# Weight-stream matmuls in groups of eight blocks instead of pairs

## The chip, the cores and the metric

The kernel runs on one core of one Trainium2 chip. The metric is the device time of one launch in microseconds, from three runs of the kernel before: median 2434.75 us (2434.34 to 2435.21).

## The reference, cut to what matters

Two layers of a decoder run over 256 tokens of width 2048, in float32. Each layer computes `h = rmsnorm(x)`, one input projection, four token mixers (softmax attention, gated short convolution, Conformer convolution, retention), an output projection, a gated MLP of width 5632 with a causal convolution of three taps, and a gated input:

```
z = h @ w_in                        # 2048 x 4928, split among the four mixers
y = concat(y_a, y_b, y_c, y_d);  x = x + y @ w_o             # 2048 x 2048
uf = dwconv(rmsnorm(x) @ w_up, w_ffn_conv)                   # 2048 x 11264
gate, up = split(uf);  x = x + (silu(gate) * up) @ w_down    # 5632 x 2048
x = x + (p @ w_pe) * sigmoid(rmsnorm(x) @ w_pg)              # 2048 x 2048
```

Every one of these products reads its weights once, since all 256 tokens fit into one pass.

## The kernel before, in words

Features lie on the partitions, tokens in the free dimension. All weights come as one stream of 128x128 blocks in the order in which TensorE takes them (`layer_plan`, line 38). The stream arrives in raw tiles of 16 blocks (queue SP, line 267, three buffers). Halves of eight blocks are converted in `conv_to` (line 260): ScalarE copies the raw float32 half to a rounded tile `hi` (line 272), VectorE subtracts to get the rest, `lo` (line 273). There are four buffers of each, and a half is converted two halves ahead of its use (`PF`, line 217).

Activations are held the same way: a tile `xs[k]` of 512 columns holds the rounded values of the 256 tokens in its first half and the rest in its second half. A product of float32 exactness is then `hi*x_hi + hi*x_lo + lo*x_hi`. With `ab` true, `linear` (line 292) does it with two matmuls for each block: `hi` against all 512 columns (a wide one) and `lo` against the first 256 columns (a narrow one), which adds into the second half of the same PSUM bank. Each of the two loads its own 128x128 block into the array first. The two halves of the bank are added when the result is evacuated (`evac`, line 339, and `x_add`, line 874).

`linear` runs over K input tiles and `nmt` output tiles (two, as a rule); the two output tiles lie in two banks of the accumulator `acc`, of which there are two. In the order before, wide and narrow alternate block by block; in the last k of a product the narrow one comes first. With `ab` false (the products of `do_up` and `w_pe`, and the last two of `w_pg`) a block takes three narrow matmuls. `linear_nat` (line 321) is another form: tokens are stationary and 512 columns of weights move, so all its matmuls are wide.

In each layer the products with `ab` true are: 17 of `w_in` (K = 16; one of them, `zkr`, has one output tile), 16 of `w_o` (K = 8, first over eight y tiles, then over the other eight), 44 of `w_up` (K = 16), 16 of `w_down` (K = 22), and seven of `w_pg` (K = 16). That makes 3152 blocks a layer.

The work of the mixers and norms is put between the matmuls of the stream as background (`Bg`, line 144): after each k `linear` calls `bg.tick()`, which advances each chain by its rate. A chain's TensorE and VectorE instructions are kept behind the stream's last instruction (`Paced`, line 122). Engines take their instructions in program order, so a background matmul that waits holds up the stream.

Of the kernel before, what the change touches and what calls it, by code (L numbers as in the profile page):

```python
# [17 lines left out]
P = 128  # L18
D = 2048
S = 256  # L20
# [13 lines left out]
CF_RATE = 0.4  # L34
HB = 8


def layer_plan():
    """Blocks of the weight stream of one layer, in the order the tensor engine takes them:
    (matrix, first row, columns)."""  # L40
    blocks = []

    def group(mat, ks, cols):
        for k in ks:
            for c in cols:
                blocks.append((mat, k * P, c))

    r = lambda a: np.arange(a, a + P)
    ks = range(KD)
    for kind, cols in in_groups():  # L50
        if kind == "up":
            up_cols = lambda h: r(h * 192)
            rope = lambda j: np.concatenate(
                [np.arange((2 * j + s) * 192 + 128, (2 * j + s) * 192 + 192) for s in (0, 1)])
            for a in (0, 2):
                group("w_kv_up", range(2), [r(h * 256) for h in (a, a + 1)])
            group("w_kv_up", range(2), [r(h * 256 + 128) for h in range(4)])
            for a in (0, 2):
                group("w_q_up", range(4), [up_cols(a), up_cols(a + 1)])
            group("w_q_up", range(4), [rope(0), rope(1)])  # L60
        else:
            group("w_in", ks, cols)
    for ys in (YORD, YLAST):
        for m in range(0, KD, 2):
            group("w_o", ys, [r(m * P), r((m + 1) * P)])
    for half in range(2):
        h0 = half * (NFF // 2)
        for j in range(h0, h0 + NFF // 2):
            group("w_up", ks, [r(j * P), r(DFF + j * P)])
        for m in range(0, KD, 2):  # L70
            group("w_down", range(h0, h0 + NFF // 2), [r(m * P), r((m + 1) * P)])
    for m in range(0, KD, 2):
        group("w_pe", range(2), [r(m * P), r((m + 1) * P)])
        if m + 2 < KD:
            group("w_pg", ks, [r(m * P), r((m + 1) * P)])
        else:
            group("w_pg", ks, [r(m * P)])
            group("w_pg", ks, [r((m + 1) * P)])
    return blocks
# [26 lines left out]

# columns of the array of per-channel vectors
def vec_plan():
# [13 lines left out]
class Paced:  # L122
    """An engine whose instructions, while the background runs, keep their place behind the
    main stream's last instruction on it."""

# [18 lines left out]
class Bg:  # L144
    """Work that is put between the groups of the main matmul stream."""

# [4 lines left out]
    def add(self, chain, rate, gen):  # L151
        """Queue gen on a chain that advances rate steps for every step of the main stream."""
        c = self.chains.setdefault(chain, [rate, deque(), 0.0])
        c[0] = rate
        c[1].append(gen)
# [30 lines left out]
def trunk(ctx: ExitStack, tc: tile.TileContext, ws, xT, pT, pos, vec, dec, ident_d, rope_c, out):  # L186
# [3 lines left out]
    V, T = Paced(tc, nc.vector, state), Paced(tc, nc.tensor, state)  # L190
# [3 lines left out]
    one = ctx.enter_context(tc.tile_pool(name="one", bufs=1))  # L194
# [16 lines left out]

# [1 line left out]
    vt = one.tile([P, L * NV], F32, tag="vt", name="vt")  # L213
# [44 lines left out]

# [1 line left out]
    def conv_to(h):  # L260
# [28 lines left out]
    bg = Bg(state)  # L289

# [1 line left out]
    def linear(xs, nmt, ab, ps=None, pre=None):  # L292
# [4 lines left out]
        else:  # L297
            t = None
        for k in range(K):
            if pre is not None:  # L300
                pre(k)
            for m in range(nmt):
                hi, lo = blk()
                f, l = k == 0, k == K - 1
                xk = xs[k]
                if ab:
                    if not l:
                        T.matmul(ps[m], hi, xk, start=f, stop=False)
                        T.anchor = T.matmul(ps[m][:, S:2 * S], lo, xk[:, 0:S], start=False, stop=False).ins
                    else:  # L310
                        T.matmul(ps[m][:, S:2 * S], lo, xk[:, 0:S], start=False, stop=False)
                        T.anchor = T.matmul(ps[m], hi, xk, start=False, stop=True).ins
                else:
                    T.matmul(ps[m][:, 0:S], hi, xk[:, 0:S], start=f, stop=False)
                    T.matmul(ps[m][:, 0:S], hi, xk[:, S:2 * S], start=False, stop=False)
                    T.anchor = T.matmul(ps[m][:, 0:S], lo, xk[:, 0:S], start=False, stop=l).ins
            bg.tick()
        return t

# [1 line left out]
    def linear_nat(xs):  # L321
# [38 lines left out]

# [1 line left out]
    def sm(n):  # L362
        return tl("s8", [P, n], F32, 24)

    def col_sums(ps, c0, srcs):
        """Sums over partitions of every [rows, S] in srcs (with the column that weighs its rows)."""
        for tt in range(2):
# [26 lines left out]
    def row_gen(hl, c0=0):  # L394
        """The values of a column pair [P, 2] (tokens on the partitions) as a row on every partition."""
        dg = tl("dg", [P, 2, 2, P], F32R, 2)
# [12 lines left out]

# [1 line left out]
    def rope_tables():  # L411
# [33 lines left out]
    def rope(dst, src, n, ct, sn, tag):  # L445
        """dst, src [P, n, S]: two heads of 64 rows on the partitions, halves of 32 rows."""
        sw = tl(tag, [P, n, S], F32, 3)
# [5 lines left out]

# [1 line left out]
    class Norm:  # L455
# [36 lines left out]
    def tiles(which, n):  # L492
        """which: 0, 1 the two sets of 16 split tiles, 2 the six spare ones."""
        return [tl("S%d_%d" % (which, i), [P, 512], F32R) for i in range(n)]
# [3 lines left out]

    # ================= one layer =================
    def layer_fwd(li, nrm, a, nxt):  # L500
        """nrm: the norm before the mixers, its split tiles in set a; nxt: set of the next layer."""
        b = 1 - a
# [7 lines left out]

# [1 line left out]
        def t_zkv(z):  # L512
# [175 lines left out]

# [1 line left out]
        cfu = [None, None]  # L690
# [49 lines left out]

# [1 line left out]
        def t_rot(z, key, sl):  # L742
# [43 lines left out]

# [1 line left out]
        scv = {}  # L788
# [81 lines left out]

# [1 line left out]
        AB = True  # L872
# [28 lines left out]

# [1 line left out]
        n3 = None  # L903
# [27 lines left out]

# [1 line left out]
        nn = norm_begin(li + 1, "g_mix", tiles(b, 16)) if li + 1 < L else None  # L933
# [31 lines left out]
def _host(inputs):  # L965
# [36 lines left out]
    vec = vec.reshape(P, L * NV)  # L1002
    # constants of the shapes
    k = np.arange(P)[:, None, None].astype(np.float64)
# [29 lines left out]
```

## Time and profile before

| what | value |
|---|---|
| median of three runs | 2434.75 us |
| span of the profiled execution | 2433.3 us |
| outside the span, against the median | about 1.45 us |
| PE busy | 2413.8 us (99%), 13808 matmuls |
| PEld busy | 2095.6 us (86%) |
| VectorE busy | 1765.3 us (73%) |
| ScalarE busy | 1321.7 us (54%) |
| HBM over the span | 181 GB/s, DMA engines 50.6% on the weight queue |

PE is TensorE's matmul row and PEld its weight loads, which overlap. The end of a matmul is modelled, and matmuls are pipelined, so the busy time of PE counts overlaps and its mean duration (394 ns for a wide one on the page) isn't what one costs. What one costs is read from the start of one to the start of the next. In a timeline row, "x2" means that two alike were merged, and the row gives the start of the first.

### The profile page before, as it was taken

What the parts mean: (1) busy time and instruction counts of PE and PEld (TensorE: products, weight loads), DVE (VectorE), ACT (ScalarE), POOL (GpSimd) and SP (SyncE); (2) the same over time, 40 slices, a digit from 0 to 9 for tenths busy, and PEclk for the clock granted to TensorE, in tenths of its full rate; (3) what the DMA queues carried; (4) which work ended last, traced back from release to release, by engine and by line L of the source; (5) the groups of instructions that cost most, each with busy time, mean ns of one, the idle gap of its engine ahead of it and who ended that gap; (6) DMA issues with size and microseconds to landing.
All of it is one profiled execution on the core that took longest, in us unless ns stands there. A gap on an engine that the chain in (4) does not pass through costs nothing.

```text
span 2433.3 us, 34793 instructions
## 1 busy us (share of the span) xinstructions
PE 2413.8 (99%) x13808; PEld 2095.6 (86%) x13808; DVE 1765.3 (73%) x2722; ACT 1321.7 (54%) x1896; POOL 11.5 (0%) x35
## 2 busy tenths in 40 slices
PE   8999999999999999999999999999999999999999
PEld 6888888888888888888888888888888888888888
DVE  7977978777556777666788788877775567776565
ACT  6665566555434555545556655655554355555453
POOL 0000000000000000000000000000000000000000
PEclk9999999999999999999999999999999999999999
DMA  6544555555555555555554445555555555555553
GB/s 245 183 147 143 190 180 184 191 191 178 188 189 190 187 179 189 191 183 182 189 185 170 149 144 189 191 186 188 181 191 190 184 184 187 190 188 181 186 200 129
DMA packets 63331, 443.33 MB, mean 182 GB/s; under 512 B 7248, under 2 KB 7504, under 8 KB 10304
## 3 DMA queue, kind: packets, MB, share of 16 engines
q1 hardware_dynamic: 62640, 439.39, 50.6%
q8 instruction: 108, 1.77, 0.3%
q0 software_dynamic: 528, 1.73, 0.2%
q14 instruction: 55, 0.45, 0.1%
HBM read 438.99 MB, written 2.10 MB: 181 GB/s over the span
## 4 chain that ended last, share of the span: by engine, by line
PE 95%; DVE 3%; ACT 1%; DMA 0%; issue 0%; SPq 0%; DVEq 0%; ACTq 0%
PE acc L133 92%; PE ps L133 3%; DVE lo L133 1%; DVE cfu L133 1%; DMA x<-xT 0%; DVE e L133 0%; ACT hi L272 0%; DVE s L133 0%; DVE m L133 0%; DVE S L133 0%; ACT dg L399 0%; DVE tabsm L133 0%; DVE tabsr L133 0%; DVE nacc L133 0%; ACT m L667 0%
## 5 line engine op out<-in xcount | busy, mean ns | idle before, releaser
L133 PE MATMUL acc<-S,hi 128*128 128x512 f32 x6560 | 2268.1, 394 | 11.5 <-DVE S L133 11.2
L133 PE MATMUL acc<-S,lo 128*128 128x256 f32 x6432 | 1777.4, 281 | 0.8 <-DVE lo L133 0.8
L133 PEld LDWEIGHTS acc<-S,hi 128*128 128x128 f32 x6560 | 1213.5, 188 | 283.3 <-DVE S L133 12.5
L133 DVE TENSOR_TENSOR lo<-raw,hi 128x1024 fp32r<-128x1024 f32 x830 | 1014.5, 1222 | 451.2 <-ACT hi L272 449.5
L133 PEld LDWEIGHTS acc<-S,lo 128*128 128x128 f32 x6432 | 1216.7, 189 | 19.7 <-DVE lo L133 1.9
L272 ACT CAST hi<-raw 128x1024 fp32r<-128x1024 f32 x830 | 869.8, 1048 | 625.4 <-PE acc L133 572.0
L342 ACT COPY e<-acc 128x512 f32<-128x512 f32 x138 | 80.5, 583 | 231.0 <-PE acc L133 231.0
L133 DVE TENSOR_TENSOR e<-acc,e 128x512 f32<-128x512 f32 x138 | 94.7, 686 | 127.7 <-ACT e L342 127.7
L133 DVE SCALAR_TENSOR_TENSOR m<-e,vt,m 128x255 f32<-128x255 f32 (+1 forms) x352 | 146.1, 477 | 0.0
L133 DVE SCALAR_TENSOR_TENSOR cfu<-cfpad,vt,cfu 128x256 f32<-128x256 f32 x240 | 115.4, 481 | 1.5
L915 ACT ACTIVATE m<-e,vt 128x256 f32<-128x256 f32 x176 | 80.1, 502 | 47.3 <-DVE e L133 47.3
L133 DVE TENSOR_TENSOR e<-e,rrow 128x512 f32<-128x512 f32 x138 | 94.7, 687 | 4.0
L877 ACT COPY e<-acc 128x512 f32<-128x512 f32 x64 | 37.5, 586 | 79.5 <-PE acc L133 79.3
L133 DVE TENSOR_TENSOR x<-x,acc 128x512 f32<-128x512 f32 x64 | 43.9, 686 | 40.3 <-ACT e L877 40.3
L920 ACT ACTIVATE m<-m 128x256 f32<-128x256 f32 x88 | 36.8, 418 | 46.7 <-DVE m L133 46.7
L133 DVE TENSOR_TENSOR x<-x,e 128x512 f32<-128x512 f32 (+1 forms) x82 | 55.6, 678 | 2.3
L133 PE MATMUL acc<-hi,S 128*128 128x512 f32 x144 | 47.1, 397 | 0.0
L357 ACT ACTIVATE S<-x,vt 128x256 fp32r<-128x256 f32 x96 | 42.9, 495 | 1.8 <-DMA x<-xT 1.8
L133 DVE SCALAR_TENSOR_TENSOR S<-x,vt,S 128x256 fp32r<-128x256 f32 x96 | 42.0, 479 | 0.9 <-ACT S L357 0.9
L133 DVE TENSOR_TENSOR S<-m,S 128x256 fp32r<-128x256 f32 x92 | 38.3, 418 | 0.0
L133 DVE TENSOR_TENSOR m<-m 128x256 f32<-128x256 f32 x90 | 37.8, 420 | 0.0
L353 ACT CAST S<-m 128x256 fp32r<-128x256 f32 x92 | 36.3, 397 | 0.0
(161 smaller groups left out, 686.9 us busy)
## 6 DMA issues: line engine op xcount, KB each, us to landing
raw<-ws SPq DMA_DIRECT2D x413, 1024.0 KB, 4.8
raw<-ws SPq DMA_DIRECT2D x4, 512.0 KB, 9.9
x<-xT SPq DMA_DIRECT2D x8, 256.0 KB, 10.5
out<-x SPq DMA_DIRECT2D x7, 256.0 KB, 2.3
dect<-dec POOLq DMA_DIRECT2D x1, 512.0 KB, 10.1
m<-pT POOLq DMA_DIRECT2D x4, 128.0 KB, 3.0
vt<-vec POOLq DMA_DIRECT2D x1, 466.0 KB, 8.6
out<-x SPq DMA_DIRECT2D x2, 128.0 KB, 1.7
```

What stands on the lines that cost most here:

```text
L133: r = fn(*a, **k)
L272: A.copy(his[i], src)
L342: A.copy(out_, t[:, 0:nmt, S:2 * S])
L353: A.copy(dst[:, 0:S], src)
L357: A.activation(dst[:, 0:S], src, AF.Identity, scale=g)
L877: A.copy(e, t[:, :, S:2 * S])
L915: A.activation(y[:, m], u[:, m], AF.Identity, scale=w(2))
L920: A.activation(y[:, 0], y[:, 0], AF.Silu)
```

## The change: groups of up to eight blocks

With `ab` true and no `pre` callback, `linear` now takes the blocks in groups of `GRP` = 8 (four k for two output tiles): first the wide matmuls of all blocks of the group, then their narrow ones. In the last group of a product the narrow ones come first. The first product of the first layer (which has a `pre`) and all products with `ab` false keep their order. The background is ticked after every `2 * nmt` matmuls, so as many times in a product as before. The number of matmuls, weight loads, conversions and DMAs stays the same.

```
+GRP = 8
...
-        for k in range(K):
+        step = GRP // nmt if ab and pre is None else 1
+        for k0 in range(0, K, step):
+            ks = range(k0, min(k0 + step, K))
             if pre is not None:
-                pre(k)
-            for m in range(nmt):
-                hi, lo = blk()
-                f, l = k == 0, k == K - 1
-                xk = xs[k]
-                if ab:
-                    if not l:
-                        T.matmul(ps[m], hi, xk, start=f, stop=False)
-                        T.anchor = T.matmul(ps[m][:, S:2 * S], lo, xk[:, 0:S], start=False, stop=False).ins
-                    else:
-                        T.matmul(ps[m][:, S:2 * S], lo, xk[:, 0:S], start=False, stop=False)
-                        T.anchor = T.matmul(ps[m], hi, xk, start=False, stop=True).ins
-                else:
+                pre(k0)
+            w = [(k, m, blk()) for k in ks for m in range(nmt)]
+            if not ab:
+                for k, m, (hi, lo) in w:
+                    f, l, xk = k == 0, k == K - 1, xs[k]
...
-            bg.tick()
+                bg.tick()
+                continue
+            last = ks[-1] == K - 1
+
+            def wide():
+                for k, m, (hi, lo) in w:
+                    yield ps[m], hi, xs[k], k == 0, k == K - 1
+
+            def narrow():
+                for k, m, (hi, lo) in w:
+                    yield ps[m][:, S:2 * S], lo, xs[k][:, 0:S], False, False
+
+            n = 0
+            for part in ((narrow, wide) if last else (wide, narrow)):
+                for o, wt, xk, f, l in part():
+                    T.anchor = T.matmul(o, wt, xk, start=f, stop=l).ins
+                    n += 1
+                    if n % (2 * nmt) == 0:
+                        bg.tick()
```

On TensorE, before, the end of a product of `w_down` (K = 22, accumulator `acc_9563`) and the start of the next read as follows. `hi` and `lo` are the halves of the weight stream, `S` the activation tiles; 128x512 is a wide matmul and 128x256 a narrow one.

```order
L133 MATMUL acc_9563<-S_4_1082_6962,hi_9616 128x512
L133 MATMUL acc_9563<-S_4_1082_6962,lo_9617 128x256
L133 MATMUL acc_9563<-S_4_1082_6962,hi_9616 128x512
L133 MATMUL acc_9563<-S_4_1082_6962,lo_9617 128x256
L133 MATMUL acc_9563<-S_5_1083_6963,lo_9617 128x256
L133 MATMUL acc_9563<-S_5_1083_6963,hi_9616 128x512
L133 MATMUL acc_9563<-S_5_1083_6963,lo_9617 128x256
L133 MATMUL acc_9563<-S_5_1083_6963,hi_9616 128x512
L133 MATMUL acc_9689<-S_0_1062_6942,hi_9636 128x512
L133 MATMUL acc_9689<-S_0_1062_6942,lo_9637 128x256
```

The same place after the change, where "x2" stands for the two output tiles:

```order
L134 MATMUL acc_9563<-S_2_1080_6960,lo_9609 128x256 x2
L134 MATMUL acc_9563<-S_3_1081_6961,lo_9609 128x256 x2
L134 MATMUL acc_9563<-S_4_1082_6962,lo_9609 128x256 x2
L134 MATMUL acc_9563<-S_5_1083_6963,lo_9609 128x256 x2
L134 MATMUL acc_9563<-S_4_1082_6962,hi_9608 128x512 x2
L134 MATMUL acc_9563<-S_5_1083_6963,hi_9608 128x512 x2
L134 MATMUL acc_9689<-S_0_1062_6942,hi_9628 128x512 x2
L134 MATMUL acc_9689<-S_1_1063_6943,hi_9628 128x512 x2
L134 MATMUL acc_9689<-S_2_1064_6944,hi_9628 128x512 x2
L134 MATMUL acc_9689<-S_3_1065_6945,hi_9628 128x512 x2
L134 MATMUL acc_9689<-S_0_1062_6942,lo_9629 128x256 x2
L134 MATMUL acc_9689<-S_1_1063_6943,lo_9629 128x256 x2
```

Wide and narrow matmuls now stand in runs, and since the last group of a product begins with the narrow ones and the next product with the wide ones, runs also meet at both ends of the last group.

On TensorE, before, where the first norm's row (`ps_315<-dg_310`, a background product of two matmuls) stands at the end of the second product of `w_in` and the start of the third:

```order
L133 MATMUL acc_327<-S_14_18_137,hi_353 128x512
L133 MATMUL acc_327<-S_14_18_137,lo_354 128x256
L133 MATMUL ps_315<-dg_310,ones_r 128x256
L133 MATMUL acc_327<-S_14_18_137,hi_353 128x512
L133 MATMUL acc_327<-S_14_18_137,lo_354 128x256
L133 MATMUL acc_327<-S_15_19_138,lo_354 128x256
L133 MATMUL acc_327<-S_15_19_138,hi_353 128x512
L133 MATMUL acc_327<-S_15_19_138,lo_354 128x256
L133 MATMUL acc_327<-S_15_19_138,hi_353 128x512
L133 MATMUL acc_427<-S_0_4_123,hi_377 128x512
L133 MATMUL ps_315<-dg_310,ones_r 128x256
L133 MATMUL acc_427<-S_0_4_123,lo_378 128x256
```

And after:

```order
L134 MATMUL acc_327<-S_14_18_137,hi_353 128x512 x2
L134 MATMUL acc_327<-S_15_19_138,hi_353 128x512 x2
L134 MATMUL acc_427<-S_0_4_123,hi_377 128x512 x2
L134 MATMUL ps_315<-dg_310,ones_r 128x256
L134 MATMUL acc_427<-S_1_5_124,hi_377 128x512 x2
L134 MATMUL ps_315<-dg_310,ones_r 128x256
L134 MATMUL acc_427<-S_2_6_125,hi_377 128x512 x2
L134 MATMUL acc_427<-S_3_7_126,hi_377 128x512 x2
L134 MATMUL acc_427<-S_0_4_123,lo_378 128x256 x2
L134 MATMUL acc_427<-S_1_5_124,lo_378 128x256 x2
```

The two background matmuls now fall into a run of wide ones, about three blocks later in the stream than before.

On ScalarE, before, around the evacuation of one product of `w_up` (`e<-acc`); `hi<-raw` is the conversion of a half, the `m` rows are the convolution and the gate, `S_10` is the rounded half of an activation tile:

```order
L272 CAST hi_8065<-raw_7985 128x1024
L342 COPY e_8049<-acc_7964 128x512
L272 CAST hi_8087<-raw_8027 128x1024
L915 ACTIVATE m_8053<-e_8049,vt 128x256 x2
L272 CAST hi_8107<-raw_8027 128x1024
L920 ACTIVATE m_8053<-m_8053 128x256
L272 CAST hi_8129<-raw_8085 128x1024
L353 CAST S_10_1072_6952<-m_8053 128x256
L272 CAST hi_8165<-raw_8085 128x1024
```

And after:

```order
L273 CAST hi_8065<-raw_7985 128x1024
L355 COPY e_8049<-acc_7964 128x512
L273 CAST hi_8087<-raw_8027 128x1024
L273 CAST hi_8107<-raw_8027 128x1024
L928 ACTIVATE m_8053<-e_8049,vt 128x256 x2
L273 CAST hi_8129<-raw_8085 128x1024
L933 ACTIVATE m_8053<-m_8053 128x256
L366 CAST S_10_1072_6952<-m_8053 128x256
L273 CAST hi_8165<-raw_8085 128x1024
```

One conversion has moved ahead of the convolution; the number of conversions that stand ahead of the evacuation is the same.

## Rows read from the trace of the kernel before

**Rows 1.** The page: span, busy times, and granted TensorE clock in 40 slices.
```profile
span 2433.3 us, 34793 instructions
...
PE 2413.8 (99%) x13808; PEld 2095.6 (86%) x13808; DVE 1765.3 (73%) x2722; ACT 1321.7 (54%) x1896; POOL 11.5 (0%) x35
...
PEclk9999999999999999999999999999999999999999
```

**Rows 2.** The page: the chain that ended last, shares by engine.
```profile
PE 95%; DVE 3%; ACT 1%; DMA 0%; issue 0%; SPq 0%; DVEq 0%; ACTq 0%
```

**Rows 3.** Waits of PE: for whom, us in total, times, longest.
```profile
PE acc L133 <- DVE S L133: 11.2, 3, 8.4
PE ps L133 <- DVE m L133: 1.0, 3, 0.6
PE ps L133 <- ACT dg L399: 0.9, 3, 0.3
PE acc L133 <- DVE lo L133: 0.8, 2, 0.6
```

**Rows 4.** Groups of instructions by shape: count, busy us, mean ns, idle before.
```profile
L133 PE MATMUL acc<-S,hi 128*128 128x512 f32 x6304 | 2221.9, 399 | 11.3 <-DVE S L133 11.2
L133 PE MATMUL acc<-S,lo 128*128 128x256 f32 x6432 | 1777.4, 281 | 0.8 <-DVE lo L133 0.8
```

**Rows 5.** The chain in order of time: start us, us, what, merged count.
```profile
254.66 27.45 PE acc L133 x156
...
385.00 734.93 PE acc L133 x4163
...
1147.65 11.31 PE acc L133 x64
...
1590.27 734.93 PE acc L133 x4163
```

**Rows 6.** Timeline of PE in a `w_up` product: start us, us, instruction.
```profile
1000.04 0.40 PE L133 MATMUL acc<-S,hi 128*128 128x512 f32 x1
1000.27 0.28 PE L133 MATMUL acc<-S,lo 128*128 128x256 f32 x1
1000.39 0.40 PE L133 MATMUL acc<-S,hi 128*128 128x512 f32 x1
...
1009.93 0.40 PE L133 MATMUL acc<-S,hi 128*128 128x512 f32 x1
```

**Rows 7.** Timeline of PE in `linear_nat` of layer one (wide matmuls alone).
```profile
172.11 0.61 PE L133 MATMUL acc<-hi,S 128*128 128x512 f32 x2
172.56 0.39 PE L133 MATMUL acc<-lo,S 128*128 128x512 f32 x1
...
175.51 0.39 PE L133 MATMUL acc<-hi,S 128*128 128x512 f32 x1
```

**Rows 8.** Timeline of PE in the last `w_pg` product (narrow matmuls alone).
```profile
2416.49 0.40 PE L133 MATMUL acc<-S,hi 128*128 128x256 f32 x2
...
2424.77 0.40 PE L133 MATMUL acc<-S,hi 128*128 128x256 f32 x2
```

**Rows 9.** Timeline of PE: wide matmuls that follow a run of narrow ones.
```profile
1312.43 0.40 PE L133 MATMUL acc<-hi,S 128*128 128x512 f32 x1
...
1312.90 0.62 PE L133 MATMUL acc<-hi,S 128*128 128x512 f32 x2
...
1314.27 0.62 PE L133 MATMUL acc<-hi,S 128*128 128x512 f32 x2
```

**Rows 10.** Timeline of PE: narrow matmuls (`w_pe`) that follow a wide one.
```profile
1119.77 0.39 PE L133 MATMUL ps<-p,hi 128*128 128x256 f32 x2
...
1120.71 0.28 PE L133 MATMUL ps<-p,lo 128*128 128x256 f32 x1
```

**Rows 11.** Timeline of PE in a `w_in` product: alternating pairs, first and last.
```profile
182.25 0.39 PE L133 MATMUL acc<-S,hi 128*128 128x512 f32 x1
...
184.68 0.39 PE L133 MATMUL acc<-S,hi 128*128 128x512 f32 x1
```

## The prediction

> **What bounds the kernel now.** I read the page first: PE is busy for 99% of the span and no other engine over 73%, and every slice of the granted clock shows 9, the top digit: the level of 2.4 GHz throughout [rows 1]. The chain that ended last lies on PE for 95% of the span [rows 2]. So I asked next what PE waits for: 11.2 us for activation tiles, with one wait of 8.4 us, which is the load of x at the start, and under 3 us for everything else, the converted weights among it [rows 3]. In the MLP the chain is PE without a break for 734.93 us in each layer [rows 5]. Weights, DMA and evacuation are hidden there; the time is the number of matmuls times the distance from one start to the next, and the change can act only through that distance or through new waits.
>
> The shapes give the number: 6304 wide matmuls with `hi`, as many as the code has blocks with `ab` true (2 x 3152), and one narrow one for each [rows 4]. Their mean times (399 and 281 ns) are modelled and overlap, so I leave them and take starts. Alternating, 28 pairs take 1009.93 - 1000.04 = 9.89 us, 353.2 ns a pair [rows 6]; over the whole MLP stage it is 734.93 / 4163 x 2 = 353.1 ns [rows 5].
>
> Then I looked for places where the kernel already does what the change will do. `linear_nat` issues wide matmuls alone, each with its own weight load: 15 of them take 175.51 - 172.11 = 3.40 us, 226.7 ns each [rows 7]. The last product of `w_pg` issues narrow ones alone: 69 take 2424.77 - 2416.49 = 8.28 us, 120.0 ns each [rows 8]. The sum is 346.7 ns, 6.4 ns less than an alternating pair costs in the MLP. Alternation isn't slow everywhere: in one product of the mixers seven pairs take 184.68 - 182.25 = 2.43 us, 347.1 ns [rows 11]. I read this as two rhythms into which an alternating stream can fall, a quick one that costs as much as the pure runs and a slow one, and nearly all of the MLP stands in the slow one. A pure run shows one steady distance alone.
>
> **What a group costs.** A run doesn't settle at once. Eight wide ones that follow narrow ones take 1314.27 - 1312.43 = 1.84 us, 0.026 more than eight settled ones (the row at 1314.27 is the ninth start) [rows 9]. Eight narrow ones right behind a wide one take 1120.71 - 1119.77 = 0.94 us, 0.02 less than eight settled ones [rows 10]. A turn from narrow to wide and back so costs 0.006 to 0.01 us net; I take 0.007. Eight blocks then cost 1.84 + 0.94 = 2.78 us against 8 x 0.3531 = 2.825. The wide runs of rows 9 are those of `linear_nat`, with tokens stationary; I assume that which operand is weights makes no difference. The bounds: without any cost of the turn 2.773; with the late start of the wide ones but no relief for the narrow ones 1.84 + 0.96 = 2.80.
>
> **The sum.** A product with K = 16 has four groups; since its last group is narrow first, it has three turns; with K = 22 (five groups and a half one) five, with K = 8 one.
>
> - `w_up`, 88 products: 32 x 0.3467 + 3 x 0.007 = 11.115 us against 32 x 0.3531 = 11.299: -0.184 each, -16.2.
> - `w_down`, 32 products of 44 pairs: 15.290 against 15.536: -0.246 each, -7.9.
> - `w_pg`, 14 products: 11.115 against 11.31 [rows 5]: -2.7.
> - `w_o`, 32 products of 16 pairs at 27.45 / 156 x 2 = 0.3519 [rows 5]: 5.554 against 5.630: -2.4.
> - `w_in`, 1088 pairs (the 32 of the first product stay): they run between 0.3471 and 0.3531, and background cuts into them. I take the middle, 0.350, against 0.3474 with turns: -2.8; the ends are +0.3 and -6.2.
>
> Together -32.0 us.
>
> **What else moves.** Nothing is added to any engine. In the last group `lo` is wanted first, so a half's VectorE result is needed where its `hi` was needed before; in all other groups it is needed 1.84 us later than now. PE waits 0.8 us for `lo` in all [rows 3], so this costs nothing. The conversion ahead of the convolution on ScalarE delays the activation tile by about one conversion; the tile is read in `w_down`, the youngest in the last group of its first product, 40 blocks (14 us) in: nothing. In `w_down` of odd number a group straddles two halves and asks for its conversion four blocks (1.4 us) early, which can only make weights earlier. The first matmuls of each product reach xs[3] after six wide ones (1.4 us) instead of 2.1, and the last four xs at block 24 instead of 24 to 30; none of the waits of rows 3 beyond the start lies there, so nothing.
>
> The background remains. Its ticks come every 0.47 us in a narrow run and every 0.92 us in a wide one, where it was 0.71. A chain that counts on some ticks between a VectorE step and its matmul gets up to 0.94 us less when four of them fall into sixteen narrow ones; behind the waiting matmul the whole stream stands. There are about 72 such places (rows of norms, transposes, value products, column sums). Waits of this kind cost 1.9 us now [rows 3]. The bounds are 0 (as many ticks come late as early) and 15 us (16 places at the full 0.94); I take +2, near to what the row shows.
>
> So the span loses 30 us: 2433.3 - 30 = 2403.3, and with the 1.45 us by which the median lies above the span, 2404.8 us, rounded 2405.
>
> **A rule against it.** Narrow runs at 120.0 ns a matmul [rows 8] are slower than narrow ones within an alternating pair, which start the next wide one after 0.12 us or a little less [rows 6]. The Trainium skill, "TensorE: Matmul & The Clock Gate", section "LDWEIGHTS (loading the stationary operand)", has a load take its column count over 1.2 GHz, some 107 ns for 128 columns (an estimate by that page); 256 columns stream in as long, so a narrow matmul has nothing to spare for the load behind it and eight in a row can't borrow from a wide neighbour. By that alone grouping would lose. The trace agrees that narrow ones don't gain, and shows that the gain is on the wide side; the sum holds both.
>
> **Rivals.**
>
> 1. *The order doesn't matter.* Each matmul costs what its columns cost, and the slow rhythm has to do with the stage, not with alternation; the groups take 353 ns a pair as well. For it: the alternating pairs of rows 11 are as quick as pure runs. Against it: no pure run in the trace settles at anything but 226.7 and 120.0, and these runs lie in both layers [rows 7 to 9]. Time: 2435. [...]
> 2. *Background waits eat the gain.* Half of the 72 places wait 0.94 us: 34 us, and 2405 - 2 + 34 = 2437. For it: the chains end within a tick or two of their use. Against it: as many ticks fall into wide runs and come late.
> 3. *Slower: the wide runs never settle.* A group has eight wide ones and the late start lasts about five; if narrow runs stay at 120.0 and restart it each time, what counts is the mean of the wide ones. From 353.1 - 120.0 = 233.1 ns on, the change loses. The first two distances together are 1312.90 - 1312.43 = 0.47 us [rows 9]; if all eight were at 236 ns, a pair costs 356 ns, and 6272 pairs x 2.9 ns = 18 us: 2453. Against it: the eight of rows 9 take 230 ns in the mean.
>
> **How the numbers follow.** Forecast 0.77, rival 1 0.06, rival 2 0.10, rival 3 0.07. The forecast's own bounds are 2395 (6272 pairs at 346.7, no turns, no waits: -40 us) and 2430 (2.80 us for each of 784 groups, -20, and 15 of waits). I take 2394 to 2430. What a measurement can't tell from no change is 0.2%, 4.9 us. Rival 2 in milder form (up to 25 us of waits) still is faster, 0.07 of its 0.10. So faster 0.84, same 0.09, slower 0.07.
>
> **What would show it.** In the MLP a product of `w_up` takes 11.1 us instead of 11.3, the uninterrupted stretch of 734.93 us shrinks to about 723, wide starts within a run stand 0.23 us apart and narrow ones 0.12, with eight of each in 2.78 us. If the MLP shrinks and the time doesn't, PE's waits for `dg`, `m` or `lo` have grown (rival 2). If wide starts stay 236 ns apart within runs, rival 3 is right, and with 353 ns a pair in either form rival 1. A MLP stretch below 715 would mean that the turns gain rather than cost, and one above 731 that my pure runs are no guide.

## The result, and the profile after

The changed kernel takes 2417.11 us (median of four runs, 2416.05 to 2419.15), the kernel before, run beside it, 2434.55 us (2433.98 to 2435.21). The ratio is 0.9929 with a 95% interval of 0.9915 to 0.9943: 17.4 us faster. The forecast was 2405 us, 30 us faster; the time lies in the range, on its slow side.

Two statements ahead of the prediction have to be corrected. The first product of layer one, which has a `pre`, doesn't keep its order: with `step` = 1 its two blocks of a k now go wide, wide, narrow, narrow. That is 32 of 6304 pairs. And the products of `w_in` with `ab` true number 18 in a layer: 17 with two output tiles, and `zkr` with one; the 3152 blocks and the 1088 pairs of the forecast count them so.

The page of the kernel after first, its span and busy times; it answers to [rows 1].

```profile
span 2416.1 us, 34796 instructions
...
PE 2392.1 (99%) x13808; PEld 2101.3 (87%) x13808; DVE 1761.2 (73%) x2722; ACT 1316.2 (54%) x1896; POOL 13.4 (1%) x35
```

The same matmuls, the same share: PE is still the engine that sets the time, and it needs 17.2 us less span for the same list. The chain of waits of the kernel after, in order of time (start, us, what), answers to [rows 5].

```profile
255.85 26.99 PE acc L134 x156
...
387.04 724.81 PE acc L134 x4158
...
1127.17 11.18 PE acc L134 x64
...
1583.49 724.84 PE acc L134 x4158
```

The MLP runs without a break in both layers, at 724.81 / 4158 x 2 = 348.6 ns a pair where it was 353.1. The prediction named about 723 us for this stretch. A product of `w_pg` takes 11.18 where it took 11.31. The stretch at 255.85 lies in the last products of the input projection of layer one and begins 1.2 us later than before: up to there the kernel has lost time.

The timeline of PE in the kernel after, in the MLP, at the end of one `w_down` product and the start of the next (start, us, instruction); the stretch answers to [rows 6].

```profile
1000.01 2.00 PE L134 MATMUL acc<-S,hi 128*128 128x512 f32 x8
1001.85 1.60 PE L134 MATMUL acc<-S,lo 128*128 128x256 f32 x12
1003.28 2.91 PE L134 MATMUL acc<-S,hi 128*128 128x512 f32 x12
1006.03 1.12 PE L134 MATMUL acc<-S,lo 128*128 128x256 f32 x8
1006.98 2.00 PE L134 MATMUL acc<-S,hi 128*128 128x512 f32 x8
1008.82 1.12 PE L134 MATMUL acc<-S,lo 128*128 128x256 f32 x8
```

The new order can be read off: eight wide, eight narrow, the last half group (four blocks) narrow first and joined to the narrow run ahead of it. Eight wide ones behind narrow ones take 1008.82 - 1006.98 = 1.84 us, just as in [rows 9]. Eight narrow ones take 1006.98 - 1006.03 = 0.95 us, where [rows 10] had given 0.94.

What PE waits for in the kernel after (for whom, us in total, times, longest), against [rows 3]:

```profile
PE acc L134 <- DVE S L134: 11.1, 3, 8.4
PE ps L134 <- ACT dg L412: 2.9, 4, 2.1
PE acc L134 <- ACT S L590: 1.5, 1, 1.5
PE acc L134 <- DVE lo L134: 1.3, 1, 1.3
PE acc L134 <- ACT hi L273: 0.8, 1, 0.8
```

The waits for the load of x, at the start, are the old ones. Behind them stand waits of 2.1, 1.5, 1.3 and 0.8 us; none of those before was longer than 0.6.

To see where the time went, I took the start of the last wide matmul of each stage in both traces and followed the difference, after less before, through both layers:

| stage, both layers | forecast, us | measured, us |
|---|---|---|
| `w_in` with the mixers | -2.8, +2 for waits | +1.6 |
| `w_o` | -2.4 | -0.6 |
| `w_up` and `w_down` | -24.1 | -17.5 |
| `w_pg` | -2.7 | -0.8 |
| sum | -30 | -17.3 |

### The profile page after: what moved, and what is told of

Its sections match the earlier page's. It is cut to its first block, busy times and chain, and to the rows that moved or that the text cites. A ratio compares the mean times of both kernels' runs of the same rounds, so it can differ in the third digit from the quotient of the medians.

```text
span 2416.1 us, 34796 instructions
## 1 busy us (share of the span) xinstructions
PE 2392.1 (99%) x13808; PEld 2101.3 (87%) x13808; DVE 1761.2 (73%) x2722; ACT 1316.2 (54%) x1896; POOL 13.4 (1%) x35
## 4 chain that ended last, share of the span: by engine, by line
PE 95%; DVE 2%; ACT 1%; DMA 1%; issue 1%; SPq 0%; DVEq 0%; ACTq 0%; POOLq 0%
PE acc L134 92%; PE ps L134 3%; DVE lo L134 1%; DVE cfu L134 0%; DMA x<-xT 0%; ACT hi L273 0%; DVE s L134 0%; DMA m<-pT 0%; ACT dg L412 0%; DVE e L134 0%; DVE m L134 0%; DVE S L134 0%; DVE tabsm L134 0%; DVE tabsr L134 0%; ACT S L370 0%
## 5 line engine op out<-in xcount | busy, mean ns | idle before, releaser
L134 PE MATMUL acc<-S,hi 128*128 128x512 f32 x6560 | 1609.1, 388 | 13.5 <-DVE S L134 11.1
L134 PEld LDWEIGHTS acc<-S,hi 128*128 128x128 f32 x6560 | 1182.0, 189 | 223.5 <-DVE S L134 11.6
L134 DVE TENSOR_TENSOR lo<-raw,hi 128x1024 fp32r<-128x1024 f32 x830 | 1003.5, 1223 | 321.2 <-ACT hi L273 204.2
L134 PEld LDWEIGHTS acc<-S,lo 128*128 128x128 f32 x6432 | 863.7, 191 | 51.4 <-issue 2.0
L134 PE MATMUL acc<-S,lo 128*128 128x256 f32 x6432 | 897.0, 283 | 1.3 <-DVE lo L134 1.3
L412 ACT ACTIVATE dg<-ident,s8r 128x128 fp32r<-128x128 f32 x104 | 33.8, 393 | 10.7 <-DVE s8r L134 10.6
```

What stands on the lines that cost most here:

```text
L134: r = fn(*a, **k)
L412: A.activation(dg[:, i, tt], ident, AF.Identity, scale=hl[i][:, c0 + tt:c0 + tt + 1])
```

## The experiments

My theory: an alternating stream can run in a slow rhythm, runs of one width can't, and a turn between the widths costs something; the background's waits take back a part. The rivals: alternation is slow for an outside reason (transfers, other engines, the PSUM bank that both matmuls of a pair write), or the loss lies in the narrow-first last k alone.

### TensorE alone, patterns of matmuls

This kernel leaves the layers out. It loads one tile of weights and tokens, and then streams matmuls in one pattern after another. The one-column matmuls that were to part the patterns all ran ahead of the first one (64 of them, from 7.34 us on), so each pattern follows the closing wide pair of the one ahead of it; the first two patterns ran partly mixed.

```
def alt(n):                       # altc
    return [(k, b, b % 2) for b in range(n) for k in "WN"]
def bankalt(n):                   # bank: the narrow one goes into the other bank
    ... out2 += [("W", b, b % 2), ("N", b, (b + 1) % 2)]
def grp(n, g): ...                # gc, ge, gi, gq: groups of 2, 4, 8, 16 blocks
```

> The layers are left out: one half of eight blocks is converted, and TensorE then issues streams of wide (512 columns) and narrow (256) matmuls on it, each with its own weight load, with nothing beside them; a pair of one-column matmuls (a gap) stands ahead of each stream. Theory (turns cost, two rhythms, all inside TensorE): wide alone settles at 226.7 ns, narrow alone at 120.0; groups of 2, 4, 8, 16 blocks cost 350.5, 350.6, 349.1, 348 ns a pair, groups of 8 with the order turned every time 348; alternating pairs cost 346.7 after a gap and 353.3 after the order of two blocks is swapped once (narrow, wide, narrow, wide), as at the end of a product; the bank that the narrow one writes makes no difference. Rival (same bank): only the stream in which the narrow matmul goes to the other bank (bank) is at 346.7, and groups of 2 are as quick as groups of 16. Rival (contention with the other engines): every stream here, alternating ones too, is at 346.7 or less.

The timeline of PE in this kernel, the first settled row and the closing row of three patterns:

```profile
145.07 2.00 PE L284 MATMUL gi<-S,hi 128*128 128x512 f32 x8
...
164.63 0.63 PE L291 MATMUL gi<-S,hi 128*128 128x512 f32 x2
...
211.34 0.40 PE L284 MATMUL bank<-S,hi 128*128 128x512 f32 x1
...
233.60 0.63 PE L291 MATMUL bank<-S,hi 128*128 128x512 f32 x2
...
265.28 0.40 PE L284 MATMUL altc<-S,hi 128*128 128x512 f32 x1
...
287.48 0.62 PE L291 MATMUL altc<-S,hi 128*128 128x512 f32 x2
```

The reader divides by the pairs between the two rows. The alternation `altc` is quick: (287.48 - 265.28) / 64 = 346.9 ns a pair. `bank` is slow: (233.60 - 211.34) / 63 = 353.3 ns. Both rates of the kernel before thus exist where VectorE does nothing, the granted clock is 1.00 (the 2.4 GHz level) and the DMA moves 1 GB/s. The rival of transfers and other engines falls. So does that of the bank: writing into two banks doesn't help, and of two further alternations into one bank alone, `one` was quick (346.7 ns) and `same`, on a single block, slow (353.4). Groups of eight take (164.63 - 145.07) / 56 = 349.3 ns here, against 348.6 in the MLP. Groups of two, from the same timeline, take 348.5, better than the 350.5 that I had expected, and groups of four, by the same reckoning, 350.8. A swap of order within an alternation, which I had thought would start the slow rhythm, was followed by a quick one; what a stream does behind a gap wasn't tried.

### Alternating, with the last k wide first too

```
-                    if not l:
...
-                    else:
-                        T.matmul(ps[m][:, S:2 * S], lo, xk[:, 0:S], start=False, stop=False)
-                        T.anchor = T.matmul(ps[m], hi, xk, start=False, stop=True).ins
+                    T.matmul(ps[m], hi, xk, start=f, stop=False)
+                    T.anchor = T.matmul(ps[m][:, S:2 * S], lo, xk[:, 0:S], start=False, stop=l).ins
```

> The kernel before, alternating, but in the last k of a product wide first as everywhere, so the stream alternates without a break from product to product. Two rhythms, of which the swap at the end of each product starts the slow one: a product of w_up takes 11.10 us instead of 11.29, the whole 2405. Rival (alternation is slow by itself, whatever stands at the ends): 2434 to 2435.

The times fall on two levels: six runs at 2421.8 to 2422.6 us, four at 2435.4 to 2435.7. The median is 2422.51, the ratio to the kernel before 0.9972 (0.9954 to 0.9991). The chain of this kernel's profiled run, one of the six shorter ones, shows where the levels come from:

```profile
386.43 733.64 PE acc L133 x4153
...
1592.40 719.80 PE acc L133 x4153
```

The two layers have the same instructions in the same order. In layer one the MLP takes 733.64 / 4153 x 2 = 353.3 ns a pair, in layer two 346.6. This is the clearest view of the two rhythms: each holds for some 720 us and more. `w_o`, just ahead of the MLP, is quick in both layers (nine products take 306.02 to 355.94 us and 1511.99 to 1561.91 us: 346.7 ns a pair). Between it and these stretches lie the places where the norm's column sums and its row, background matmuls, cut into the first two products of `w_up`; there the rhythm of layer one turned slow. The 13.8 us between the two stretches are about the 13.2 us between the two levels of time, so I take the four longer ones to have both layers slow, but none of them was profiled: that isn't shown. The swap in the last k is not what makes the rhythm slow, since layer one is slow without it. My 2405 us, with all stages quick, was missed.

### Groups of two, groups of sixteen

```
-GRP = 8
+GRP = 2
```

> Groups of two blocks (one k): wide, wide, narrow, narrow. Cost by turns, from the first distances of the runs in the changed kernel (two wide 233 + 236, two narrow 113 + 119): 350.5 ns a pair, 2418 to 2420. Rival (what counts is that a narrow matmul doesn't stand behind its own wide one in the same bank, the size of the group is nothing): the same as groups of eight, 2417. Rival (gain in proportion to turns saved, 7 in 8 for groups of eight, half for groups of two): 2425.

2412.15 us (2412.07 to 2412.26), ratio 0.9909 (0.9893 to 0.9926): faster than groups of eight, against my expectation. Its chain and its waits of PE:

```profile
382.95 726.40 PE acc L134 x4164
...
1576.88 726.40 PE acc L134 x4164
```

```profile
PE acc L134 <- DVE S L134: 10.6, 2, 8.7
PE ps L134 <- DVE m L134: 0.9, 1, 0.9
```

The MLP gains nearly as much as with groups of eight (348.9 ns a pair against 348.6), and the long waits are not there. The 5 us between the two kernels come from the waits, not from the MLP's matmuls: all waits of PE add up to 13.0 us here and to 18.2 in the changed kernel.

```
-GRP = 8
+GRP = 16
...
-        step = GRP // nmt if ab and pre is None else 1
+        step = min(GRP // nmt, K // 2) if ab and pre is None else 1
```

> Groups of sixteen blocks (eight for K = 8 and for zkr), so one turn in a product with K = 16 instead of three and two with K = 22 instead of five. Cost by turns (20 ns each, 600 before, some 230 now): 2417 - 7 = 2410. Rival (the group's size is nothing): 2417. Rival (the stream waits for its conversions, since sixteen blocks hold two of four buffers): over 2420, with PE's waits for lo and hi grown from 2 us.

2408.23 us (2407.97 to 2408.60), ratio 0.9893 (0.9878 to 0.9908). Its chain:

```profile
383.66 722.12 PE acc L134 x4158
...
1577.01 722.12 PE acc L134 x4158
```

This is the test of the turn's price. With settled pairs at 346.7 ns the 2079 pairs of the stretch take 720.8 us. Groups of eight have 44 x 3 + 16 x 5 = 212 turns in it and lie 4.0 us above, 19 ns a turn. Groups of sixteen have 44 x 1 + 16 x 2 = 76 turns and lie 1.3 us above, 17 ns. Single products agree: from end to end one of `w_up` takes 11.153 us in groups of eight and 11.113 in groups of sixteen, and 11.093 in the quick layer of the run above, 60 ns more for three turns and 20 for one. The prediction had 7 ns.

The group in the input projection was sixteen as well. Against the kernel before, by the starts of the last wide matmuls, it gained 2.3 us there in layer one and lost 1.0 in layer two; groups of eight lost 0.9 and 0.7.

### The input projection in groups of two, the rest in groups of eight

```
-    def linear(xs, nmt, ab, ps=None, pre=None):
+    def linear(xs, nmt, ab, ps=None, pre=None, small=False):
...
-        step = GRP // nmt if ab and pre is None else 1
+        step = GRP // nmt if ab and pre is None and not small else 1
...
-            t = linear(h, n, AB_IN, pre=pre)
+            t = linear(h, n, AB_IN, pre=pre, small=True)
```

> Groups of eight everywhere but in the input projection, which has groups of two. Theory (the groups of eight in the input projection crowd the background and add some 6 us of waits there; the streams of the output projection and MLP gain 0.15 to 0.19 us a product as before): the mixers of groups of two with the MLP of groups of eight, 2410 to 2412. Rival (the extra waits are not from there, or they are the scheduler's chance anywhere): 2416 to 2418.

2412.76 us (2412.53 to 2413.09), ratio 0.9911 (0.9896 to 0.9926). The MLP is that of the changed kernel; the waits of PE are as short as with groups of two; the row for `dg`:

```profile
PE ps L134 <- ACT dg L412: 1.0, 4, 0.3
```

By the reckoning of the table above, `w_in` now brings -1.5 us in layer one and -1.4 in layer two, where the changed kernel lost 0.9 and 0.7. So the groups of eight in the input projection cost 4.6 us against groups of two, and it is shown that they do it there. That it is their size isn't: groups of sixteen gained 1.3 us there in both layers together.

### The loads of p ahead of the output projection

In the changed kernel the longest new wait stands in layer two. Its timeline of ScalarE:

```profile
1433.86 0.41 ACT L366 CAST p<-m 128x256 fp32r<-128x256 f32 x1 [4.32 <-DMA m<-pT]
1434.18 0.58 ACT L355 COPY e<-acc 128x512 f32<-128x512 f32 x1
...
1438.76 1.28 ACT L412 ACTIVATE dg<-ident,s8r 128x128 fp32r<-128x128 f32 x4
```

and that of PE:

```profile
1439.50 0.38 PE L134 MATMUL ps<-dg,ones_r 128*128 128x256 f32 x1 [2.13 <-ACT dg L412]
```

ScalarE stands 4.32 us for the second load of `p`, which is issued at 1427.73 us and takes 6.1 us to land. Both loads take buffers of the tag `m`, which the background uses too; I read the late issue as a wait for a buffer. The evacuation of an accumulator and the `dg` row stand behind it in program order, and PE waits 2.13 us for `dg`. The experiment issues the loads ahead of the output projection, into two buffers of tiles that are free by then:

```
-            sq = tl("krsq", [64, S], F32)
+            sq = tl("krsq", [P, 1, S], F32)[0:64, 0]
...
+        praw = [tl("kr", [P, 1, S], F32), tl("krsq", [P, 1, S], F32)]
+        for k in range(2):
+            nc.gpsimd.dma_start(praw[k], pT[li, k][:, None, :])
...
-            raw = tl("m", [P, S], F32, 3)
-            nc.gpsimd.dma_start(raw, pT[li, k])
...
-            split(t, raw)
+            split(t, praw[k][:, 0])
```

> Groups of eight as in the changed kernel, but the two tiles of p are loaded into buffers of their own instead of two of the three that the mixers use, before the output projection. Theory (2.3 us of the second layer's loss is ScalarE, which stands 4.3 us before the load of p has landed, and with it the evacuation and the retention's row behind it): the step at the product sb0 of layer two goes, 2414 to 2415. Rival (that wait is hidden anyway, the row is late for another reason): 2417.

2416.43 us (2415.47 to 2417.44), ratio 0.9926 (0.9911 to 0.9941). In the trace it does what it should; a row of the waits of PE:

```profile
PE ps L134 <- ACT dg L412: 0.8, 3, 0.3
```

The long wait for `dg` is gone (2.1 us before, now at most 0.3), and the span of the profiled run is 2.3 us shorter. In the time, the 0.7 us between the medians lie within the spread of the runs: inconclusive there.

### Widths and beginnings, TensorE alone

The layers are left out here as well. Each pattern streams 48 matmuls of one width, or an alternation behind different beginnings:

```
for n, nm_ in ((512, "wa"), (448, "wb"), (384, "wc"), (320, "wd"), (256, "we"), (192, "wf"), ...):
    widths(nm_, [n] * 48)
... ra: two wide ones, then alternating;  rb: two wide, one narrow, then alternating
```

> The layers are left out; TensorE alone issues runs of matmuls of one width (512, 448, 384, 320, 256, 192, 128, 64 columns), three alternations of two widths, and ten alternations of 512 and 256 columns behind different beginnings (0 to 4 narrow matmuls, 2 to 6 wide ones). Theory: each matmul with a weight load of its own costs its columns at 2.4 GHz plus a fixed 13.3 ns (226.7 - 213.3, 120.0 - 106.7): 200.0, 173.3, 146.7 ns for 448, 384, 320 columns; at 192 columns and fewer the weight load takes over, so the distance stays at some floor near 112 ns, the distance of one-column matmuls. Rival (the cost above the columns is in proportion, 17/16): 198.3, 170.0, 141.7, and 113.3 for 256. Alternations behind different beginnings: if the rhythm is set by where a stream begins, some of the ten run at 346.7 ns a pair and some at 353.3 from their first pairs to their last; if it were drawn anew on the way, single streams would change it.

The timeline of PE in this kernel, with the row that follows each width, and then the first and the last row of two alternations:

```profile
69.25 7.20 PE L326 MATMUL wd<-S,hi 128*128 128x320 f32 x48
76.29 0.63 PE L328 MATMUL wd<-S,hi 128*128 128x512 f32 x2
...
83.89 5.50 PE L326 MATMUL wf<-S,hi 128*128 128x192 f32 x48
89.23 0.64 PE L328 MATMUL wf<-S,hi 128*128 128x512 f32 x2
...
140.96 0.40 PE L284 MATMUL ra<-S,hi 128*128 128x512 f32 x1
...
154.74 0.63 PE L291 MATMUL ra<-S,hi 128*128 128x512 f32 x2
155.79 0.39 PE L284 MATMUL rb<-S,hi 128*128 128x512 f32 x1
...
169.66 0.62 PE L291 MATMUL rb<-S,hi 128*128 128x512 f32 x2
```

320 columns: (76.29 - 69.25) / 48 = 146.7 ns; 192 columns: 111.3 ns. 384 columns take 173.3 ns over the second half of their run, and 128 columns stand near 111 as well. 448 columns never settle at one distance: to the end of the run it moves between 198 and 208 ns, 202.7 in the mean, so the 200.0 expected there is missed.

The two alternations differ in one narrow matmul at the beginning: `ra` takes 13.78 us for 39 pairs, 353.3 ns, `rb` 13.87 us for 40 pairs, 346.8 ns, and each keeps its rhythm to its end. So do the other eight:

| beginning, then alternating from a wide one | ns a pair |
|---|---|
| 2 wide (`ra`, `rf`) | 353.3, 353.3 |
| 2 wide, then 1, 2, 3, 4 narrow (`rb` to `re`) | 346.8, 346.5, 353.3, 346.8 |
| 3, 4, 5, 6 wide (`rg` to `rj`) | 353.3 each |

No single stream changed on the way, as the theory had it. The two rhythms differ in their period too: from one wide matmul to the next, `ra` repeats 350, 350 and 360 ns, and `rb` 350 and 344. But the order at the beginning doesn't settle the matter alone. In the first program of matmul patterns `nfirst` issues the same widths in the same order as `rb`, two wide, one narrow and then alternating, on other blocks and banks:

```profile
288.51 0.39 PE L284 MATMUL nfirst<-S,hi 128*128 128x512 f32 x1
...
310.77 0.40 PE L284 MATMUL nfirst<-S,hi 128*128 128x512 f32 x1
```

It takes (310.77 - 288.51) / 63 = 353.3 ns a pair, and `rb` 346.8. What else counts, the state in which the stream ahead left the engine or the operands, isn't known.

### The parts together

Groups of two in `w_in`, groups of sixteen elsewhere, and the early loads of `p`; the diff joins those of the three experiments above.

> Groups of two in the input projection, of sixteen in all other products (eight where K is 8), and the loads of p as in e5. Cost by turns: w_up -0.19, w_down -0.25, w_pg -0.17 us a product against before as in e3, mixers as in e2 (-2 us in each layer): 2434.4 - 32 = 2402 to 2404. Rival (gains of the two don't add, since waits move elsewhere): 2408 or more.

2405.84 us (2405.70 to 2405.89 in three runs; a fourth took 6096.06 us and isn't counted), ratio 0.9883 (0.9863 to 0.9902). It beats both kernels, 11 us under the changed one, and misses the 2402 to 2404 expected by 2 us. Its waits of PE, beyond the load of x, come to 1.5 us for `m`, 0.7 for `e` and 0.3 for `lo`.

## Why the prediction was right, and where it was too high

**The two distances.** Right. Wide ones in runs settle at 226.7 ns and narrow ones at 120.0, in the MLP as in [rows 7, 8], and the eight wide ones behind narrow ones take the 1.84 us of [rows 9], though there the tokens were the weights. The assumption that this makes no difference held.

**The two rhythms.** Right, and more than an inference now: both appear in one program with nothing beside TensorE, and in two layers of one kernel. The kernel before had its MLP in the slow one.

**The turn.** This is the term of the sum that was mis-sized. The relief of the narrow run was read as 0.02 us from [rows 10]. Measured are 0.953 us for eight narrow ones against 0.960 settled: 0.007. The row was taken behind an alternating stretch, whose last wide matmul took 230 ns and not the settled 227; the narrow distances behind it are 113, 117, 118 and 119 ns, and behind a settled wide run 113 and then 120. So a turn costs 27 - 7 = 20 ns and not 7. At 498 turns in `w_up`, `w_down`, `w_o` and `w_pg` that is 13 x 498 = 6.5 us, half of the 12.7 us that are missing. The rest, by the table and the paragraphs below: some 2.4 us in `w_in`, 2.4 at seams between products, and 1.4 in `w_o` beyond its turns. The upper bound, 2.80 us a group, was the better value.

**`w_o`.** The 0.3519 us a pair comes from a misread row. The stretch of 27.45 us in [rows 5] ends at 282.11 us, and the first matmul of `w_o` starts at 283.08: it belongs to the last three products of `w_in`. In `w_o` itself the kernel before shows, at two ends of products (the last wide matmul of one and the first of the next):

```profile
311.50 0.62 PE L133 MATMUL acc<-S,hi 128*128 128x512 f32 x2
...
361.94 0.62 PE L133 MATMUL acc<-S,hi 128*128 128x512 f32 x2
```

Between them lie nine products, 50.44 us, 0.3503 a pair: they take 5.64 and 5.56 us by turns, so every second one ran quick. With turns of 20 ns, -0.04 us a product are left, not -0.076.

**`w_in`.** The rate term was too small, in the good direction. An undisturbed product of it lost 0.15 us, what one of `w_up` lost: these stood in the slow rhythm, as the misread row had shown with its 0.3519, and [rows 11] shows an exception.

**Conversions "cost nothing".** Wrong in one place. ScalarE in the kernel after, while the products `zq1` and `do_up` of layer one run:

```profile
94.32 0.51 ACT L550 ACTIVATE m<-e,vt 128x256 f32<-128x256 f32 x1
...
96.01 1.24 ACT L462 COPY m<-m 32x256 f32<-32x256 f32 x3
...
98.61 2.92 ACT L273 CAST hi<-raw 128x1024 fp32r<-128x1024 f32 x3
```

Ten background instructions stand in a row ahead of three conversions. In the kernel before, two conversions lay between the same instructions:

```profile
95.79 1.04 ACT L272 CAST hi<-raw 128x1024 fp32r<-128x1024 f32 x1
...
98.53 1.06 ACT L272 CAST hi<-raw 128x1024 fp32r<-128x1024 f32 x1
```

The timeline of PE in the kernel after, in the same stretch:

```profile
99.69 0.51 PE L134 MATMUL acc<-S,hi 128*128 128x256 f32 x2 [0.83 <-ACT hi L273]
101.54 1.22 PE L134 MATMUL acc<-S,lo 128*128 128x256 f32 x8 [1.34 <-DVE lo L134]
...
107.30 0.51 PE L134 MATMUL acc<-S,hi 128*128 128x256 f32 x2 [1.51 <-ACT S L590]
```

PE waits for `hi`, then for the `lo` made from it. The prediction asked whether a weight is wanted earlier, and it mostly isn't. It didn't ask what stands ahead of the conversion on ScalarE when a group takes eight blocks at once. My account is that a group asks for its conversions in one place of the program, and the background's ScalarE work gathers between such places. It isn't shown as a rule of the size: with groups of sixteen a conversion lies between these instructions again,

```profile
97.23 1.05 ACT L273 CAST hi<-raw 128x1024 fp32r<-128x1024 f32 x1
```

and PE's waits for `hi` and `lo` at this place are gone.

**The background's waits.** Forecast +2 us, measured 4.6 in `w_in` (the difference to the kernel with groups of two there). Rival 2 was thus partly true, as a mechanism and not in its size. It named as the source VectorE steps that end a tick too late; the traces show work standing in program order on ScalarE, once behind a late load, once behind gathered background work.

**Rivals 1 and 3.** Rival 1 falls: the order does matter, 348.6 against 353.1 ns in the MLP. A part of it holds, though: alternation as such isn't slow, since in its quick rhythm it costs 346.6 ns in the same stage, less than the groups. The Trainium skill, "TensorE: Matmul & The Clock Gate", section "Back-to-back issue gap", gives columns over 2.4 GHz plus 2.5 ns for the gap of a matmul alone, and says that in a stream of weight loads and matmuls both set the distance. The runs here agree that the formula isn't enough for such a stream: above the columns stand 13.3 ns, not 2.5, in the settled runs of 512, 384, 320 and 256 columns. Rival 3 falls as well: eight wide ones take 230 ns in the mean, not 236.

**What stays open.** Some 2.4 us were lost at seams, against what the other products of the same kind gained: about 0.5 us a layer at the first `w_pg` product, 0.3 of it a wait of PE for `dg`, and 0.7 at the first two `w_up` products, where the trace names no wait. Why TensorE has two stable rhythms of alternation isn't known, nor what selects one: the beginning of a stream has a part in it, but its order alone doesn't fix it. Nor is it known why groups of four are dearer than groups of two.

## What to carry to other kernels

When one engine is busy all the time, read its price as the distance from start to start, and for each pattern separately: the same instructions here cost 346.7 or 353.3 ns a pair, depending on the rhythm that the stream had fallen into. Groups of eight cost 348.6 in both layers: 4.5 less than the slow alternation that this kernel happened to stand in, and 2 more than a quick one would have cost. They are worth having where the rhythm can't be chosen. Take the price of a turn from a place where both runs are long, since a run measured behind a mixed stretch starts from another state. When work is issued in larger groups, ask what now stands ahead of each conversion or load on the in-order engines that feed the stream, and try the size of the group where background work is dense: in the input projection here groups of eight lost 1.6 us against the order before, while groups of two gained 2.9 and groups of sixteen 1.3.

## What the runs showed of the hardware

- An alternation of 512- and 256-column matmuls, each with its own weight load, has two stable rhythms, 346.7 and 353.3 ns a pair at the granted clock of 1.00. Streams that differed in one narrow matmul at the beginning took different ones, but two with the same order of widths did so as well. One held for over 700 us. In one kernel the MLP of layer one ran slow and that of layer two quick, and its times fell on two levels 13 us apart.
- Settled runs of one width cost the columns at 2.4 GHz and 13.3 ns (226.7, 173.3, 146.7 and 120.0 ns for 512, 384, 320 and 256 columns; 448 columns didn't settle and took 202.7 in the mean), but not less than about 111 ns (111.3 at 192 columns, the like at 128). The Trainium skill, "TensorE: Matmul & The Clock Gate", section "LDWEIGHTS (loading the stationary operand)", has a load take its columns over 1.2 GHz, for 128 columns 107 ns (an estimate by that page); the floor measured here lies near it.
- A turn from a narrow run to a wide one and back costs 20 ns against settled runs, in the pattern `gi`: eight wide matmuls behind narrow ones take 1841 ns instead of 1814, eight narrow ones behind wide ones 953 instead of 960.
